# A late start for the second norm's spread over the partitions: behind the first half of FFN-in's first doubled pair

## The chip, the cores and the metric

One core of a Trainium2 chip runs the whole layer in one launch. The metric is the device time of one execution in microseconds. A profile shows one execution; its span runs from the first to the last instruction on the core, and the device time is a little longer than the span.

## The reference

One decoder layer, with 512 tokens of width 2048, in float32. The last part of it matters here:

```python
x = x + merged @ w_o[i]

h = rmsnorm(x, ffn_norm_g[i])
hid = h @ w_ffn_in[i]
gate = hid[..., :FFN_HIDDEN]
up = hid[..., FFN_HIDDEN:]
x = x + (jax.nn.silu(gate) * up) @ w_ffn_out[i]
```

`rmsnorm` divides each token by the root of its mean square and multiplies by a gain for each column. FFN_HIDDEN is 5632, so `w_ffn_in` is 2048 by 11264.

## The kernel before, in words

Everything lies transposed: the partitions hold model columns, the free dimension holds the 512 tokens. A float32 product is made of three products of rounded operands: each operand is split into a high part (ScalarE, L266 for activations and L334 for weights) and a low part, what the rounding left over (VectorE, L267 and L331). TensorE then multiplies high by high, high by low and low by high (`mm3`, L271 to L273).

A `Pair` (L572) is an output of 256 columns by 512 tokens. It comes in kinds. A **plain** pair multiplies eight operands of 256 rows ("forms", 0 to 7) with `mm3`, 12 matmuls for each form, into two PSUM banks, which L716 copies out. A **doubled** pair does the same job by a scheme with seven products instead of eight blocks: each product is one 512-column matmul of the high weights (L623, the activation's high and low halves side by side) and one 256-column matmul of the low weights (L625). Its weights come in four tiles of two forms each, 28 matmuls for each tile. It has seven PSUM accumulators: six banks named `ps` and one named `small`. `mix_doubled` (L671) adds the seven up on ScalarE and VectorE, at lines L680 and L683. There are two banks named `small`; the norm's work and the attention use them too.

Weights land by DMA in five landing buffers. SP's queue issues two loads for each weight tile (L316, L318), GpSimd's queue adds a third onto the first (L338, an accumulating load), VectorE makes two sums (L350), and the L334 and L331 splits write into one of three weight slots (`whi_76`, `whi_78`, `whi_80` and their `wlo`). A slot is written again when TensorE has done with it.

FFN-in has 44 pairs, `m` = 0 to 43 (L1302). Pair 0 is plain, pairs 1 to 43 are doubled. The forms of pair 0 are made while it runs: each is loaded from the spilled stream (L479, the transfer `wholes<-x`), multiplied by the gain (L483), and split for the plain pair (L266, L267), while L497 and two more splits make the further blocks that a doubled pair needs.

The norm's factor for each token is not applied to the forms but to the results: `hidden` (L1292) multiplies the gate half by `row2` (L1294), takes Silu (L1295), multiplies by the up half (L1297) and stores. `row2` is the factor of each token, the same in every partition. `Norm` (L861) makes it: squares are summed over the tiles, four small matmuls sum over the partitions (L882), VectorE and GpSimd make mean and power of minus one half (L887, L890), with the tokens on the partitions. Then `spread` (L849) turns these into a row in every partition: for each of four groups of 128 tokens VectorE writes a diagonal matrix (L854, two buffers), and TensorE multiplies it by ones (L856). L896 copies the PSUM bank to `row2`. A float32 matmul at L856 shows as two passes in the trace, so the four make eight.

The order is written by the recording program: `tick` (L198) runs after each group of matmuls, counts a clock, and runs whatever `after` (L192) has queued for that count. A `Staged` generator does one step at each tick. The scheduler then lays out each engine's instructions by priority and readiness. `norm2.row()` (L1305) ends whatever is left of the norm's steps at once.

Of the kernel before, what the change touches and what calls it, by code (L numbers as in the profile page):

```python
# [65 lines left out]
def hybrid_layer(  # L66
# [28 lines left out]
    def nm(s):  # L95
        return f"{s}_{next(names)}"
# [3 lines left out]
    class Block:  # L100
        def __init__(self, arena, start, n):
            self.arena, self.start, self.n = arena, start, n
# [8 lines left out]
    class Arena:  # L111
# [5 lines left out]
        def take(self, n, how="low"):  # L117


            spots = []  # L120
            for start, size in self.holes:
                end = start + size
                if how == "place":
                    start = -(-start // PLACE) * PLACE
                if end - start >= n:
                    if how == "high":
                        spots.append((-end, end - n))
                    elif how != "old":
                        spots.append((start, start))
                    else:  # L130
                        spots.extend((self.given[a // P : -(-(a + n) // P)].max(), a)
                                     for a in {*range(start, end - n + 1, 256), end - n})
            at = min(spots)[1]
            start, size = next(h for h in self.holes if h[0] <= at < h[0] + h[1])
            self.holes.remove((start, size))
            self.holes.extend(
                h for h in ((start, at - start), (at + n, start + size - at - n)) if h[1])
            return Block(self, at, n)

        def give(self, block):  # L140
            self.turns += 1
            self.given[block.start // P : -(-(block.start + block.n) // P)] = self.turns
            holes = sorted(self.holes + [(block.start, block.n)])
            self.holes = holes[:1]
            for s, n in holes[1:]:
                if sum(self.holes[-1]) == s:
                    self.holes[-1] = (self.holes[-1][0], self.holes[-1][1] + n)
                else:
                    self.holes.append((s, n))
# [26 lines left out]
    def small_bank():  # L176
        return psa.tile([P, T], F32, tag="small", name=nm("small"))
# [14 lines left out]
    def after(n, fn):  # L192
        heapq.heappush(waiting, (clock[0] + n, next(names), fn))
# [109 lines left out]
    class Weights:  # L303
# [20 lines left out]
        def steps(self):  # L324
            raw, c = self.blocks(self.land.f()), LANDED[self.kind]
            s = self.blocks(summed.f(), 2)

            def split(lo, blocks, r):
                h = self.hi[:, blocks]
                if lo:  # L330
                    in_turn(nc.vector.tensor_tensor(out=self.lo[:, blocks], in0=r,  # L331
                                                    in1=h.bitcast(F32), op=ALU.subtract))
                else:
                    in_turn(nc.scalar.activation(h, r, AF.Copy))  # L334

            def landed():
                if self.kind == "S":
                    nc.gpsimd.dma_start(out=raw[:, 3:5], in_=self.src[:, 1:3], accum_op=ALU.add)  # L338

            def high():  # L340
                self.slot = slots.popleft()
                self.hi, self.lo = (self.blocks(t, 7 if self.kind == "S" else 4)
                                    for t in self.slot)
                split(False, slice(0, c), raw)

            def sums():
                if self.kind == "S":
                    for o, x, y in ((s[:, 0], raw[:, 3], raw[:, 1]),
                                    (s[:, 1], s[:, 0], raw[:, 2])):
                        in_turn(nc.vector.tensor_tensor(out=o, in0=x, in1=y, op=ALU.add))  # L350

            def rest():
                split(True, slice(0, c), raw)
                if self.kind == "S":
                    split(False, slice(5, 7), s)
                    split(True, slice(5, 7), s)
                if spare[0] < 0:
                    spare[0] += 1
                    give(self.land)
                else:  # L360
                    landings.append(self.land)

            return landed, high, sums, rest
# [15 lines left out]
    def next_weights():  # L379
        ahead(1)  # L380
        return prepared.popleft().get()
# [20 lines left out]
    def doubles(kinds, at=0):  # L402

        k = 0
        while k < len(kinds):
            n = 2 if (at + k) % 2 == 0 and kinds[k : k + 2] in ("SS", "PP") else 1
            yield k, n
            k += n
# [325 lines left out]
    def pair(forms, last=False, plain=False, parts_done=None, at=0, home=lambda: None,  # L734
             doubled=False):

        kinds = "P" * len(forms) if plain else "".join(f.kind for f in forms)
        p = Pair(kinds, home, doubled)
        for k, n in doubles(kinds, at):
            slot, ws = next_weights()  # L740
            fs = forms[k : k + n]
            p.add("P" if plain else fs[0].kind, ws, [f.plain() if plain else f.get() for f in fs])
            for f in fs:
                if plain:
                    f.use_plain()
                if last:
                    f.free()
            slots.append(slot)
            if parts_done and k + n == kinds.find("P"):
                last_parts(p, forms[k + n :], parts_done)  # L750
                break
        return p

    def last_parts(p, forms, done):


        ws = [(f.get(), w) for k, n in doubles("P" * len(forms), len(GATE) - len(forms))
              for f, w in zip(forms[k : k + n], next_weights()[1])]
        y, z = p.ends()
        for ps, bs, a, b, c in ((y, (2, 3), 0, T, 0), (z[:, :256], (0, 1), 0, 256, T),  # L760
                                (bank()[:, :256], (0, 1), 256, T, T)):
            for u, ((xh, xl), (wh, wl)) in enumerate(ws):
                for k, i in enumerate(bs):
                    mm3(ps, wh[:, i], wl[:, i], xh[k][:, a:b], xl[k][:, a:b],
                        c + a > T and u + k == 0, k == 1 and u == len(ws) - 1)
            done(p.o, c + a, c + b, ps)
# [92 lines left out]


    class Norm:  # L861
        def __init__(self):
            self.acc = take(T)
            self.done = 0

        def add(self, raw):
            sq, acc = wide(), self.acc.f()
# [11 lines left out]
        def steps(self):  # L879
            ps = small_bank()  # L880
            for t in range(NT):
                nc.tensor.matmul(ps[:, t : t + 1], self.acc.f(t * P, (t + 1) * P), ones[:, 0:1],  # L882
                                 start=True, stop=True)
            give(self.acc)
            yield
            self.mean = consts.tile([P, NT], F32, name=nm("mean"))
            nc.vector.tensor_scalar(out=self.mean, in0=ps[:, :NT], scalar1=1.0 / D, scalar2=EPS,  # L887
                                    op0=ALU.mult, op1=ALU.add)
            self.cols = consts.tile([P, NT], F32, name=nm("cols"))
            nc.gpsimd.tensor_tensor(out=self.cols, in0=self.mean, in1=expo[:, :NT], op=ALU.pow)  # L890
            for _ in range(3):
                yield
            ps = spread(self.cols)
            yield
            self.block = take(T)
            nc.scalar.activation(self.block.f(), ps, AF.Copy)  # L896
            return self.block.f()
# [293 lines left out]
    for n, ((w, i), pr) in enumerate(zip(order, made())):  # L1191
# [6 lines left out]
        o = pr.out(block(w, i) if n < 3 else None)  # L1198
# [52 lines left out]
    give(norm1.block)  # L1251


    norm2 = Norm()
    spill = {(n, j): tc.dram_tile([P, 1024], F32, name=nm(n)) for n in ("x1", "sum", "x2")
             for j in range(KU)}
    there = set()
# [34 lines left out]
    def hidden(m, o):  # L1292
        g = o[:, :T]
        nc.vector.tensor_tensor(out=g, in0=g, in1=row2, op=ALU.mult)  # L1294
        nc.scalar.activation(g, g, AF.Silu)  # L1295
        yield
        nc.vector.tensor_tensor(out=g, in0=g, in1=o[:, T:], op=ALU.mult)  # L1297
        nc.sync.dma_start(out=spill["hid", m // 2][:, (m % 2) * T : (m % 2 + 1) * T], in_=g)
        if m % 2 == 1:
            there.add(("hid", m // 2))  # L1300

    for m in range(KH):  # L1302
        o = pair(fs, last=m == KH - 1, plain=m == 0, doubled=True).out()
        if m == 0:
            row2 = norm2.row()  # L1305
        st = Staged(hidden(m, o))
        st.step()
        if m == KH - 1:
            st.get()

# [29 lines left out]
    for j in range(KU):  # L1340
# [22 lines left out]
        else:  # L1363
            o = pair(gs, plain=j == 0).out()
# [90 lines left out]
```

## Time and profile before

| what | value |
|---|---|
| median of 3 runs | 2733.71 us |
| the three runs | 2729.75, 2733.71, 2735.45 us |
| profiled execution, device time | 2732.84 us |
| its span | 2731.1 us |
| granted TensorE clock, mean | 0.998 |
| instructions | 45752 |

TensorE is shown busy in nearly the whole span. Matmul durations in the trace include their drain (0.39 us for 512 columns), so the distance between the starts of two matmuls says how fast they go, not the duration. In the rows below, a number in square brackets is the idle time of the engine before the row, with what ended it.

### The profile page before, as it was taken

The page shows a single profiled execution, that of the slowest core. Times are in us where ns is not written, and L with a number is a line of the kernel's source. Part 1 is how long each engine was busy: PE and PEld are TensorE (multiplying, and loading weights), DVE is VectorE, ACT ScalarE, POOL GpSimd, SP SyncE. Part 2 cuts the span into 40 slices and gives each one's busy share as a digit, 9 for nine tenths or more (in the row PEclk, how much of TensorE's full clock was granted, in tenths as well). Part 3 has the DMA queues.
Part 4 walks back from the last instruction along what each step waited for, and adds up shares of the span by engine and source line. Part 5 has one row for each costly group of instructions (what it writes and reads, how often), then busy time and mean ns, then how long its engine had stood idle before and what let it go on. Part 6 is the DMA issues. An engine that isn't in the chain of part 4 may idle for free.

```text
span 2731.1 us, 45752 instructions
## 1 busy us (share of the span) xinstructions
PE 2703.8 (99%) x17243; PEld 2442.1 (89%) x17243; DVE 2073.4 (76%) x3377; ACT 1353.8 (50%) x2045; POOL 447.7 (16%) x527
## 2 busy tenths in 40 slices
PE   9999999999999999999999999999999999999999
PEld 7899999999998889988888888888888999989898
DVE  8566767677776567678888888888889567778776
ACT  7645556555554334364444444444445344453543
POOL 0222323232220000001111111111111111111110
PEclk9999999999999999999999999999999999999999
DMA  7677676777775457667888788888877659688784
GB/s 226 154 179 174 172 173 170 182 172 184 179 191 184 147 149 224 193 195 198 221 201 207 197 200 203 197 197 201 202 194 213 180 166 268 183 248 243 232 232 118
DMA packets 303134, 529.05 MB, mean 194 GB/s; under 512 B 25664, under 2 KB 162880, under 8 KB 302912
## 3 DMA queue, kind: packets, MB, share of 16 engines
q1 hardware_dynamic: 242160, 425.70, 49.0%
q0 software_dynamic: 60752, 100.43, 23.5%
q8 instruction: 135, 2.21, 0.3%
q14 instruction: 87, 0.71, 0.1%
HBM read 478.84 MB, written 47.19 MB: 193 GB/s over the span
## 4 chain that ended last, share of the span: by engine, by line
PE 93%; DMA 2%; DVE 2%; ACT 1%; issue 1%; POOL 0%; SPq 0%; ACTq 0%; DVEq 0%; POOLq 0%
PE ps L272 20%; PE ps L273 20%; PE ps L271 20%; PE ps L623 18%; PE ps L625 9%; PE small L623 3%; PE small L625 1%; PE small L1050 1%; PE small L942 1%; PE small L1026 1%; PE small L1003 1%; DMA wholes<-w_first 1%; DMA ple<-out 0%; DVE wlo L331 0%; DMA wholes<-x 0%
## 5 line engine op out<-in xcount | busy, mean ns | idle before, releaser
L271 PE MATMUL ps<-parts,whi 128*128 128x256 f32 (+1 forms) x3995 | 1245.0, 313 | 15.4 <-ACT parts L266 7.6
L334 ACT ACTIVATE whi<-wholes 128x512 fp32r<-128x512 f32 (+4 forms) x950 | 856.3, 917 | 792.5 <-PE ps L272 315.7
L272 PE MATMUL ps<-parts,whi 128*128 128x256 f32 (+1 forms) x3960 | 1229.8, 311 | 1.3 <-DVE parts L267 1.3
L273 PE MATMUL ps<-parts,wlo 128*128 128x256 f32 (+1 forms) x3960 | 1228.7, 310 | 0.1
L331 DVE TENSOR_TENSOR wlo<-wholes,whi 128x512 fp32r<-128x512 f32 (+4 forms) x950 | 964.1, 1048 | 154.9 <-ACT whi L334 153.5
L271 PEld LDWEIGHTS ps<-parts,whi 128*128 128x128 f32 x3995 | 763.4, 191 | 63.8 <-ACT parts L266 7.8
L272 PEld LDWEIGHTS ps<-parts,whi 128*128 128x128 f32 x3960 | 756.9, 191 | 44.8 <-DVE parts L267 2.2
L273 PEld LDWEIGHTS ps<-parts,wlo 128*128 128x128 f32 x3960 | 756.6, 191 | 39.2 <-DVE wlo L331 1.1
L623 PE MATMUL ps<-parts,whi 128*128 128x512 f32 x2064 | 739.0, 399 | 0.0
L625 PE MATMUL ps<-parts,wlo 128*128 128x256 f32 x2064 | 579.7, 281 | 0.0
L623 PEld LDWEIGHTS ps<-parts,whi 128*128 128x128 f32 x2064 | 387.8, 188 | 96.9
L625 PEld LDWEIGHTS ps<-parts,wlo 128*128 128x128 f32 x2064 | 389.9, 189 | 0.0
L350 DVE TENSOR_TENSOR wholes<-wholes 128x256 f32<-128x256 f32 (+1 forms) x794 | 328.2, 413 | 22.1 <-DMA wholes<-w_ffn_out 2.4
L338 POOL DMA_DIRECT2D wholes<-w_ffn_in x172 | 149.7, 870 | 699.2 <-DVE wholes L350 266.6
L338 POOL DMA_DIRECT2D wholes<-w_in x132 | 117.3, 891 | 516.0 <-DMA wholes<-w_in 248.1
L683 DVE TENSOR_TENSOR out<-out,ps 128x256 f32<-128x256 f32 x258 | 107.2, 416 | 94.5 <-ACT out L680 94.4
L652 DVE TENSOR_TENSOR out<-out 128x256 f32<-128x256 f32 x59 | 25.0, 424 | 180.6 <-ACT out L649 180.3
L267 DVE TENSOR_TENSOR parts<-wholes,parts 128x1024 fp32r<-128x1024 f32 (+4 forms) x131 | 123.6, 952 | 13.9 <-ACT parts L266 13.6
L623 PE MATMUL small<-parts,whi 128*128 128x512 f32 x344 | 131.2, 399 | 0.0
L266 ACT ACTIVATE parts<-wholes 128x1024 fp32r<-128x1024 f32 (+4 forms) x131 | 105.6, 834 | 38.9 <-DVE wholes L497 18.1
L338 POOL DMA_DIRECT2D wholes<-w_ffn_out x56 | 57.0, 1036 | 401.8 <-DMA wholes<-w_ffn_out 190.3
L1295 ACT ACTIVATE out<-out 128x512 f32<-128x512 f32 x44 | 27.8, 633 | 165.4 <-DVE out L1294 165.4
(119 smaller groups left out, 1666.9 us busy)
## 6 DMA issues: line engine op xcount, KB each, us to landing
wholes<-w_ffn_in SPq DMA_DIRECT2D x172, 384.0 KB, 5.4
wholes<-w_in SPq DMA_DIRECT2D x132, 384.0 KB, 4.8
wholes<-w_ffn_in SPq DMA_DIRECT2D x172, 256.0 KB, 4.6
wholes<-w_ffn_in POOLq DMA_DIRECT2D x172, 256.0 KB, 5.2
wholes<-w_in SPq DMA_DIRECT2D x132, 256.0 KB, 3.9
wholes<-w_in POOLq DMA_DIRECT2D x132, 256.0 KB, 4.8
wholes<-x SPq DMA_DIRECT2D x32, 512.0 KB, 5.3
wholes<-w_ffn_out SPq DMA_DIRECT2D x31, 512.0 KB, 4.3
```

The lines of the kernel that those rows point to most:

```text
L266: return (nc.scalar.activation(hi, src, AF.Copy), nc.vector.tensor_tensor(out=lo, in0=src, in1=hi.bitcast(F32), op=ALU.subtract))
L267: nc.vector.tensor_tensor(out=lo, in0=src, in1=hi.bitcast(F32), op=ALU.subtract))
L271: nc.tensor.matmul(ps[:, s], sh, mh[:, s], start=start, stop=False)
L272: nc.tensor.matmul(ps, sh, ml, start=False, stop=False)
L273: return nc.tensor.matmul(ps, sl, mh, start=False, stop=stop)
L331: in_turn(nc.vector.tensor_tensor(out=self.lo[:, blocks], in0=r, in1=h.bitcast(F32), op=ALU.subtract))
L334: in_turn(nc.scalar.activation(h, r, AF.Copy))
L338: nc.gpsimd.dma_start(out=raw[:, 3:5], in_=self.src[:, 1:3], accum_op=ALU.add)
L350: in_turn(nc.vector.tensor_tensor(out=o, in0=x, in1=y, op=ALU.add))
L623: nc.tensor.matmul(ps, wh[:, w], t[:, x].rearrange("p s c -> p (s c)"), start=first, stop=False)
L625: mark(nc.tensor.matmul(ps[:, :256], wl[:, w], t[:, x, 0], start=False, stop=last))
L683: in_turn(nc.vector.tensor_tensor(out=out, in0=x, in1=y, op=op))
```

## The change

The second norm is made with `held=True`, and its generator stops ahead of `spread` for as long as that holds. It is let go by `first_out`, four ticks after pair 0 has been read out. `row2` and the first step of `hidden` for pair 0 follow there.

```diff
     class Norm:
-        def __init__(self):
+        def __init__(self, held=False):
             self.acc = take(T)
-            self.done = 0
+            self.done, self.held = 0, held
...
             for _ in range(3):
                 yield
+            while self.held:
+                yield
             ps = spread(self.cols)
...
-    norm2 = Norm()
+    norm2 = Norm(held=True)
...
+    def first_out():
+        nonlocal row2
+        norm2.held = False
+        row2 = norm2.row()
+        st.step()
+
+    row2 = None
     for m in range(KH):
         o = pair(fs, last=m == KH - 1, plain=m == 0, doubled=True).out()
+        st = Staged(hidden(m, o))
         if m == 0:
-            row2 = norm2.row()
-        st = Staged(hidden(m, o))
-        st.step()
+            after(4, first_out)
+        else:
+            st.step()
```

The engines' orders in the two built programs are the same up to the old place of the spread and again from the end of pair 1 on; instructions and addresses are the same there. Between the two, TensorE's order is (shortened; names without numbers; T1 to T4 are the four weight tiles of pair 1):

```
before                                     changed
pair 0, forms 0, 1 (24 matmuls)            pair 0, forms 0, 1 (24)
L856 x2, one L271, L856 x2                 -
pair 0, forms 2 to 7 (72)                  pair 0, forms 2 to 6 (60)
                                           pair 1, T1: one L623
                                           pair 0, form 7: two L271
                                           pair 1, T1: L625, L623, ... (8)
                                           pair 0, form 7: the other ten
pair 1, T1 (28)                            pair 1, T1: the other 19
pair 1, T2 (28)                            pair 1, T2 (28)
                                           L856 x2, T3: one L623, L856 x2
pair 1, T3, T4                             pair 1, T3 (its L625 next), T4
```

On ScalarE, the two L334 of T2 stood behind form 7's first L266 and stand ahead of it in the changed program (L483 x2, L334 x2, L266). On VectorE, T2's two L331 likewise stand ahead of form 7's first L267. The four L854 stand behind the L331 of T4, with an L350 behind the first and another behind the second. The store of pair 0's hidden half moves on SP's queue behind two more sets of weight loads.

## Prediction, made before the changed kernel ran

> **What bounds the kernel now.** I read the page first, then the stretches around the change, then the engines' orders there in time.
>
> ```profile
> span 2731.1 us, 45752 instructions
> PE 2703.8 (99%) x17243; PEld 2442.1 (89%) x17243; DVE 2073.4 (76%) x3377; ACT 1353.8 (50%) x2045; POOL 447.7 (16%) x527
> ```
>
> TensorE sets the end: whatever it waits for here is added to the time, whatever it stops waiting for is taken off, until a place where it waits for something else. Its busy share counts drains, so the speed is read from the starts of matmuls. The first fence of starts is the plain pair, then the first doubled one:
>
> ```profile
> 1217.28 0.39 PE L271 MATMUL ps<-parts,whi 128*128 128x512 f32 x1
> ...
> 1225.44 0.39 PE L271 MATMUL ps<-parts,whi 128*128 128x512 f32 x1
> 1225.67 0.48 PE L272 MATMUL ps<-parts,whi 128*128 128x512 f32 x1
> ...
> 1228.30 0.39 PE L623 MATMUL ps<-parts,whi 128*128 128x512 f32 x1
> ...
> 1238.18 0.40 PE L623 MATMUL ps<-parts,whi 128*128 128x512 f32 x1
> ```
>
> 36 matmuls lie between the first two rows: 8.16/36 = 0.227 us for each of 512 columns. Between the last two lie two weight tiles of 28 matmuls: 9.88/28 = 0.353 us for a couple of L623 and L625. The row at 1225.44 is the first matmul of form 7, the last form of pair 0; 1228.30 is the first of T1 (pair 1's first weight tile), 1238.18 the first of T3.
>
> What the spread costs at its old place:
>
> ```profile
> 1210.15 0.39 PE L273 MATMUL ps<-parts,wlo 128*128 128x512 f32 x1
> 1210.38 0.60 PE L856 MATMUL small<-diag,ones 128*128 128x128 f32 x4
> 1210.74 0.48 PE L271 MATMUL ps<-parts,whi 128*128 128x512 f32 x1
> 1211.47 0.71 PE L856 MATMUL small<-diag,ones 128*128 128x128 f32 x4 [0.25 <-DVE diag L854]
> 1211.94 0.48 PE L272 MATMUL ps<-parts,whi 128*128 128x512 f32 x1
> 1212.25 0.40 PE L273 MATMUL ps<-parts,wlo 128*128 128x512 f32 x1
> ```
>
> From 1210.15 to 1212.25 are 2.10 us, in which three matmuls would have taken 0.68: the spread costs **1.42 us** of TensorE. Half a microsecond of it is the wait for the third diagonal, which VectorE made late behind a split:
>
> ```profile
> 1210.00 1.22 DVE L267 TENSOR_TENSOR parts<-wholes,parts 128x1024 fp32r<-128x1024 f32 x1
> 1211.14 0.47 DVE L854 TENSOR_SCALAR diag<-ident,cols 128x128 f32<-128x128 f32 x2
> ```
>
> **The change part by part.**
>
> *Removed at the old place:* 1.42 us of TensorE. Without more, form 7 would be reached at 1225.44 - 1.42 = 1224.02.
>
> *What is late next: form 7.* Its raw tile comes by DMA:
>
> ```profile
> 1213.76 0.42 SPq L479 DMA_DIRECT2D wholes<-x  x1
> 1221.88 1.34 ACT L483 ACTIVATE wholes<-wholes,gcol 128x512 f32<-128x512 f32 x2 [2.22 <-DMA wholes<-x]
> 1223.25 1.06 ACT L266 ACTIVATE parts<-wholes 128x1024 fp32r<-128x1024 f32 x1
> 1224.22 1.77 ACT L334 ACTIVATE whi<-wholes 128x1280 fp32r<-128x1280 f32 x2
> 1224.39 1.22 DVE L267 TENSOR_TENSOR parts<-wholes,parts 128x1024 fp32r<-128x1024 f32 x1
> 1225.52 2.09 DVE L331 TENSOR_TENSOR wlo<-wholes,whi 128x1280 fp32r<-128x1280 f32 x2
> 1225.90 1.44 ACT L266 ACTIVATE parts<-wholes 128x768 fp32r<-128x768 f32 x3
> ```
>
> and the stretch in which it was under way (after the engines: granted clock, DMA share, GB/s):
>
> ```profile
> 1213.00:1220.00 7.00, 7.00 (x32) 5.78 (x31) 3.74 (x7) 2.65 (x5) 1.75 (x2) 1.00 1.07 347
> ```
>
> The tile was asked for at 1213.76 and landed at 1221.88, in a stretch where the DMA engines were busy all the time (share 1.07, 347 GB/s). This does not follow TensorE: nothing that the change removes lies ahead of that load except 1.1 us of VectorE work, and the split that releases the two loads in front of it waits for ScalarE anyway. I take 1221.88 as it is. Already before, TensorE came 0.2 us too early: the L272 above at 1225.67 starts when VectorE's L267 (1224.39 + 1.22) is done. So of the 1.42 us at most that much could have been won if nothing else were touched.
>
> The changed order is worse there. ScalarE does L483, then both L334 of T2, and only then form 7's high split. L334 takes 1.68 us from start to the next start (1224.22 to 1225.90) and can follow L483 at 1223.15, so L266 runs from 1224.85 to 1225.9. TensorE's order is one product of T1, then form 7's two L271. It reaches the first of these at 1224.02 + 0.23 = 1224.25, finds no high part, and stands until 1225.95: **1.7 us of waiting**, for what was 0.2. The T1 products that lie behind in its order are ready and can't go first. VectorE's low split of form 7 is behind T2's two L331: these can follow L334's first half at about 1224.45 and take 2.0, then L267 1.22, done at 1227.65. TensorE asks for it after two L271 and four couples, 1225.95 + 0.45 + 1.41 = 1227.8: no wait.
>
> *On to the new place.* From 1225.95 twelve matmuls of form 7 (2.72), 27 couples and one L625 (9.65) are left ahead of T3: 1238.3. I add 0.15 for a bank: pair 1's sixth accumulator takes over pair 0's second bank, which is copied out behind the two L334 of T3, here as before:
>
> ```profile
> 1228.27 1.88 ACT L334 ACTIVATE whi<-wholes 128x1280 fp32r<-128x1280 f32 x2 [0.45 <-PE ps L272]
> 1230.06 0.58 ACT L716 ACTIVATE out<-ps 128x512 f32<-128x512 f32 x1
> 1230.65 1.28 ACT L1295 ACT_TABLE_LOAD   x1
> 1231.95 0.63 ACT L1295 ACTIVATE out<-out 128x512 f32<-128x512 f32 x1
> ```
>
> In the new order the L334 start when pair 0's last L272 drains (1230.0), the copy ends 1.79 + 0.58 later, at 1232.4, and TensorE wants the bank at 1232.3. So T3 is reached at **1238.45**, against 1238.18 before.
>
> *The spread at the new place.* The rows that make it:
>
> ```profile
> L854 DVE TENSOR_SCALAR diag<-ident,cols x12: 278/280/389, 69.4 to 2578.0; 128x128 f32<-128x128 f32 x12
> L856 PE MATMUL small<-diag,ones x24: 270/275/377, 76.3 to 2579.4; 128*128 128x128 f32 x24
> 1234.20 2.09 DVE L331 TENSOR_TENSOR wlo<-wholes,whi 128x1280 fp32r<-128x1280 f32 x2
> 1236.54 0.88 DVE L350 TENSOR_TENSOR wholes<-wholes 128x256 f32<-128x256 f32 x2
> ```
>
> VectorE has the first diagonal behind T4's L331. With form 7 and T3's splits 1 us later than before, I get these L331 from 1234.7 to 1236.75 (before: the third row, 1234.20 to 1236.29), and diagonals 1 and 2, with an L350 of 0.34 between, by 1237.6. TensorE, at 1238.45, need not wait. The first two L856 take 0.36 (1210.38 to 1210.74), the L623 0.23. Diagonal 3 has to wait for the first L856 to read its buffer (two buffers, as before), about 0.37 after it starts; then 0.28 for itself and some 0.05 for each of two signals: ready at 0.75, when TensorE has been at 0.59 for a moment; diagonal 4 follows at 0.95, the last L856 takes 0.18, and the weights behind it come some 0.08 late, as at 1212.25. That is 1.2 us, of which 0.23 is the L623: **0.97 us**. Bounds: 0.9 without a wait (0.36 + 0.47 + 0.08, from the old place), 1.42 as it was. I take 0.97, since the late split on VectorE is gone, but the hand-over of the diagonals is not.
>
> *Behind the new waits.* While VectorE waits for the third diagonal's buffer, the L331 of pair 2's first tile (2.0 us) stand behind it, wanted only after T3 and T4, 9.9 us later. ScalarE's copy to `row2`, the table load and Silu end near 1242.3; behind them stands an L334 that waits for T3's last products anyway, near 1243.8: hidden, 1.5 us to spare. The store of the hidden half leaves SP near 1243.5 instead of 1233.97; its buffer is wanted again by pair 2's sums, over 10 us on. GpSimd's queue has its loads in the same order. These go at nothing.
>
> **Sum.** 0.27 us late at T3, and 0.97 for the spread: **+1.24 us**. Behind that everything follows TensorE as before. The profiled execution took 2732.84 us (span 2731.1 and 1.7 around it), so 2734.1. The median of the three runs lies 0.9 above the profiled execution (range 2729.75 to 2735.45); from there the same sum is 2734.95. A difference below 0.2% (5.5 us) is about what can't be told from no change here.
>
> **The rivals.**
>
> *Form 7 is in time.* If its tile lands 1.7 us earlier in most executions, the wait at its L271 is gone, and the change only exchanges 1.42 for 0.97: -0.45, and -0.2 for the wait that was there before: 2732.2. For it: other executions differ by 5 us. Against it: the DMA share over 1 at a fixed place. 18%.
>
> *VectorE is late at the new place.* The diagonals now stand behind T4's splits and an L350, with 0.85 us to spare by my sum. If the chain through form 7 is later by 1 to 3 us, TensorE stands at L856 for the excess of it, one for one: about +1 more, 2735.1 and up to 2736.5. 12%.
>
> *Slower: the tile lands later and TensorE cools.* T1's splits come 1.4 us earlier, so SP sends the next two weight loads at 1218.6 and not at the row below, while form 7's tile is still on its way:
>
> ```profile
> 1220.08 0.38 SPq L316 DMA_DIRECT2D wholes<-w_ffn_in  x1
> 1202.63 0.39 PE L273 MATMUL ps<-parts,wlo 128*128 128x512 f32 x1
> 1203.87 0.50 PE L271 MATMUL ps<-parts,whi 128*128 128x512 f32 x1 [0.85 <-ACT out L802]
> ```
>
> The two are 640 KB, at 347 GB/s 1.9 us; at worst the tile is that much later, and TensorE's gap grows from 1.7 to 3.6 us. The trace's own gap of 0.85 us, at 1203, left the next matmuls at 0.23 apart; no gap of this stage is longer. If from about twice that on the clock is halved for as long as the gap lasted, 1.8 to 3.6 us of matmuls are lost again, say 2.6: 1.24 + 1.9 + 2.6 = +5.7, 2738.5. [...] 8%.
>
> That the spread isn't where it is meant to be is ruled out by the built order.
>
> **How the numbers follow.** Forecast 62%, 2734.1, by itself 2732.5 to 2736. The rivals add 2732.2 below and 2738.5 above; the runs' own spread is -4.0 and +1.7 about their median. Eight times in ten: 2730.5 to 2738.5. Beyond 0.2% lie only the slower rival's upper half and runs that scatter: faster 0.04, same 0.89, slower 0.07.
>
> **What would show it.** In the changed profile: form 7's first L271 with about 1.7 us of idle time, released by ScalarE's L266; L334 between L483 and L266; the eight L856 near 1239 with a wait below 0.3 us and no L267 ahead of the third diagonal; the granted clock at 1.00; T3's next products at 0.35 us a couple. Wrong would be: the tile `wholes<-x` landing elsewhere than near 1222, idle time at the first L856, or a change of idle time anywhere behind 1245.

## The result, and the profile after

| | before | after |
|---|---|---|
| median | 2733.23 us of 20 runs (2728.1 to 2738.55) | 2727.74 us of 20 runs (2716.0 to 2737.29) |
| ratio after / before | | 0.9974, 95% interval 0.9962 to 0.9985 |
| profiled execution | 2732.84 us | 2727.78 us |

The changed kernel is 0.26% faster where 0.05% slower was forecast, and the time lies below the range. The second thing to see in the table is the scatter: 10 us for the kernel before, 21 us for the changed one, with six of its twenty executions between 2716 and 2719.1 and only one more below 2725.

The span and L623, the 512-column product of a couple, on the page of after:

```profile
span 2726.1 us, 45750 instructions
L623 PE MATMUL ps<-parts,whi 128*128 128x512 f32 x2064 | 726.7, 392 | 0.0
```

and L623 on the page of before:

```profile
L623 PE MATMUL ps<-parts,whi 128*128 128x512 f32 x2064 | 739.0, 399 | 0.0
```

The number of these instructions is the same, no idle time stands on either line (the last column), and yet L623 takes 392 ns instead of 399. Only the starts of matmuls tell what that is worth. The timeline answers three places of each kernel: the last L273 ahead of the old place of the spread (for before it stands in the prediction, 1210.15), the first L623 of pair 2, and the last L623 of FFN-in. Before:

```profile
1248.07 0.40 PE L623 MATMUL ps<-parts,whi 128*128 128x512 f32 x1
2078.76 0.40 PE L623 MATMUL small<-parts,whi 128*128 128x512 f32 x1
```

After:

```profile
1213.98 0.39 PE L273 MATMUL ps<-parts,wlo 128*128 128x512 f32 x1
1255.26 0.39 PE L623 MATMUL ps<-parts,whi 128*128 128x512 f32 x1
2070.36 0.39 PE L623 MATMUL small<-parts,whi 128*128 128x512 f32 x1
```

- Up to the old place this execution is 3.83 us later than that of before. Nothing is changed there: it is scatter of the earlier stages.
- From there to pair 2 before took 37.92 us, after 41.28. So the stretch that the change touches became **3.36 us longer**; the forecast was +1.24.
- From pair 2 to the end of FFN-in before took 830.69 us and after 815.10: **15.6 us shorter**, in a stretch where both kernels issue the same instructions in the same order. FFN-in has 2408 couples of L623 and L625 (2064 + 344, the 344 into the small bank), 14 to a weight tile and 56 to a pair; 2351 of them lie between these rows. 830.69/2351 = 0.3533 us for a couple, 815.10/2351 = 0.3467.
- Behind FFN-in the lead shrinks from 8.4 to 5.0 us (the spans), again in work that nothing changed.

The 15.6 us don't come in one place. A window of before (time, busy time and number of instructions of each engine, granted clock, DMA share, GB/s):

```profile
1250.00:1500.00 250.00, 250.00 (x1418) 216.78 (x1416) 219.69 (x394) 117.34 (x163) 43.52 (x50) 1.00 0.83 207
```

and two of after:

```profile
1250.00:1500.00 250.00, 250.00 (x1444) 220.68 (x1443) 222.48 (x400) 121.00 (x169) 44.37 (x51) 1.00 0.83 209
1750.00:2000.00 250.00, 250.00 (x1445) 220.66 (x1444) 222.58 (x401) 120.43 (x168) 45.29 (x52) 1.00 0.83 206
```

TensorE is busy 250 us of 250 and has a granted clock of 1.00 in all three, and does 1444 matmuls in the one kernel and 1418 in the other. Busy share and clock hide the difference; the count shows it.

In the timeline the two look like this. Before:

```profile
1300.01 0.40 PE L623 MATMUL ps<-parts,whi 128*128 128x512 f32 x1
1300.25 0.28 PE L625 MATMUL ps<-parts,wlo 128*128 128x256 f32 x1
1300.37 0.40 PE L623 MATMUL ps<-parts,whi 128*128 128x512 f32 x1
...
1301.07 0.40 PE L623 MATMUL ps<-parts,whi 128*128 128x512 f32 x1
```

After:

```profile
1299.98 0.39 PE L623 MATMUL ps<-parts,whi 128*128 128x512 f32 x1
1300.21 0.28 PE L625 MATMUL ps<-parts,wlo 128*128 128x256 f32 x1
1300.33 0.39 PE L623 MATMUL ps<-parts,whi 128*128 128x512 f32 x1
...
1301.02 0.39 PE L623 MATMUL ps<-parts,whi 128*128 128x512 f32 x1
```

From the first row to the last are three couples: 1.06 us before, 1.04 after. In nanoseconds, before repeats every three couples: from an L623 to its L625 241, 236, 233, and from there to the next L623 120, 113, 117; 353 a couple. After is even, 230 and 117, 347 a couple. I call them the **slow** and the **quick rhythm**. Before has the slow one in all of its couples; after has it through T2 and the quick one from the spread on (a few couples of T1 ran at 347 ns too).

That gives the theory to test (R): the couples have two stable rhythms; which one runs is set by the last thing that disturbed the stream, and it then lasts for hundreds of couples. The spread's last matmuls, in front of a 256-column product, turned it. Rivals: the long stall at form 7 turned it (C); any small matmul in the stream would (P); the gain comes from the place that the spread left (W).

### The profile page after: what moved, and what is told of

Its sections match the earlier page's. It is cut to its first block, busy times and chain, and to the rows that moved or that the text cites. A ratio compares the mean times of both kernels' runs of the same rounds, so it can differ in the third digit from the quotient of the medians.

```text
span 2726.1 us, 45750 instructions
## 1 busy us (share of the span) xinstructions
PE 2691.6 (99%) x17243; PEld 2443.3 (90%) x17243; DVE 2072.4 (76%) x3377; ACT 1353.3 (50%) x2045; POOL 448.3 (16%) x527
## 4 chain that ended last, share of the span: by engine, by line
PE 90%; issue 3%; DMA 2%; DVE 2%; ACT 1%; POOL 1%; SPq 0%; DVEq 0%; ACTq 0%; POOLq 0%
PE ps L273 19%; PE ps L272 19%; PE ps L271 19%; PE ps L623 17%; PE ps L625 9%; PE small L623 3%; PE small L625 1%; DVE wlo L331 1%; DMA wholes<-x 1%; PE small L1052 1%; PE small L1028 1%; PE small L1005 1%; PE small L944 1%; ACT whi L334 0%; DMA wholes<-w_in 0%
## 5 line engine op out<-in xcount | busy, mean ns | idle before, releaser
L271 PE MATMUL ps<-parts,whi 128*128 128x256 f32 (+1 forms) x3995 | 1247.5, 314 | 18.5 <-ACT parts L266 10.2
L334 ACT ACTIVATE whi<-wholes 128x512 fp32r<-128x512 f32 (+4 forms) x950 | 855.6, 917 | 782.0 <-PE ps L272 307.8
L272 PE MATMUL ps<-parts,whi 128*128 128x256 f32 (+1 forms) x3960 | 1231.8, 311 | 1.3 <-DVE parts L267 1.3
L273 PE MATMUL ps<-parts,wlo 128*128 128x256 f32 (+1 forms) x3960 | 1230.5, 311 | 1.7 <-DVE wlo L331 1.5
L331 DVE TENSOR_TENSOR wlo<-wholes,whi 128x512 fp32r<-128x512 f32 (+4 forms) x950 | 964.0, 1049 | 157.8 <-ACT whi L334 156.3
L271 PEld LDWEIGHTS ps<-parts,whi 128*128 128x128 f32 x3995 | 764.4, 191 | 68.1 <-ACT parts L266 11.1
L272 PEld LDWEIGHTS ps<-parts,whi 128*128 128x128 f32 x3960 | 758.0, 191 | 44.8 <-DVE parts L267 2.4
L273 PEld LDWEIGHTS ps<-parts,wlo 128*128 128x128 f32 x3960 | 757.8, 191 | 40.8 <-DVE wlo L331 2.7
L623 PE MATMUL ps<-parts,whi 128*128 128x512 f32 x2064 | 726.7, 392 | 0.0
L625 PE MATMUL ps<-parts,wlo 128*128 128x256 f32 x2064 | 579.6, 281 | 0.0
L623 PEld LDWEIGHTS ps<-parts,whi 128*128 128x128 f32 x2064 | 386.7, 187 | 84.5 <-ACT out L716 0.3
L625 PEld LDWEIGHTS ps<-parts,wlo 128*128 128x128 f32 x2064 | 391.3, 190 | 0.1
L350 DVE TENSOR_TENSOR wholes<-wholes 128x256 f32<-128x256 f32 (+1 forms) x794 | 329.0, 414 | 27.7 <-DMA wholes<-w_ffn_out 4.6
L683 DVE TENSOR_TENSOR out<-out,ps 128x256 f32<-128x256 f32 x258 | 107.5, 417 | 77.9 <-ACT out L680 77.8
L267 DVE TENSOR_TENSOR parts<-wholes,parts 128x1024 fp32r<-128x1024 f32 (+4 forms) x131 | 123.7, 954 | 16.0 <-ACT parts L266 15.7
L623 PE MATMUL small<-parts,whi 128*128 128x512 f32 x344 | 128.8, 391 | 0.0
L266 ACT ACTIVATE parts<-wholes 128x1024 fp32r<-128x1024 f32 (+4 forms) x131 | 105.5, 834 | 42.2 <-DVE wholes L497 16.7
```

Source lines behind the costliest of these rows:

```text
L266: return (nc.scalar.activation(hi, src, AF.Copy), nc.vector.tensor_tensor(out=lo, in0=src, in1=hi.bitcast(F32), op=ALU.subtract))
L267: nc.vector.tensor_tensor(out=lo, in0=src, in1=hi.bitcast(F32), op=ALU.subtract))
L271: nc.tensor.matmul(ps[:, s], sh, mh[:, s], start=start, stop=False)
L272: nc.tensor.matmul(ps, sh, ml, start=False, stop=False)
L273: return nc.tensor.matmul(ps, sl, mh, start=False, stop=stop)
L623: nc.tensor.matmul(ps, wh[:, w], t[:, x].rearrange("p s c -> p (s c)"), start=first, stop=False)
```

## The experiments

All times are medians, with the range and the number of executions, beside runs of before on the same chip. Lines inserted into the kernels move the couple's L623 and L625 to L633 and L637 (or a line or two off). The small matmul of the experiments is

```
def tap():
    nc.tensor.matmul(small_bank()[:, :P], ones, ident, start=True, stop=True)
```

and nothing reads its result; everything else is computed as before. `self.number` counts the doubled pairs from 1, `self.tile` a pair's weight tiles from 0; i is the product, u the couple in it.

**1. One small matmul in front of a 256-column product, in the kernel before.**

```diff
                         nc.tensor.matmul(ps, wh[:, w], t[:, x]...)
+                        if self.number == 1 and self.tile == 2 and i == 0 and u == 0:
+                            tap()
                         mark(nc.tensor.matmul(ps[:, :256], wl[:, w], t[:, x, 0], ...))
```

> The kernel before with the spread at its old place and one more small matmul (128 columns, ident and ones into a spare bank, its result unread), put between the first 512-column product and the first 256-column product of the third tile of the first doubled pair. Theory R (the couples of the doubled product have two rhythms, 353 and 347 ns, and a small matmul in front of a 256-column product puts them into the quick one for the rest of FFN-in): 347 ns per couple from that place on, no stall at form 7 beyond 0.2 us, no half clock there; 2733.2 - 15.7 + 0.2 = about 2718 us. Rival C (the quick rhythm comes from the 2.2 us stall and the half clock at form 7, which this kernel does not have): 353 ns, 2733.5 us. Rival W (the gain comes from taking the spread out of the stretch behind the plain pair): 353 ns, 2733.5 us.

Measured: 2727.97 us (2719.43 to 2730.49, 8 runs; before 2733.49), ratio 0.9975 (0.9965 to 0.9985). The spread is at its old place, and the rhythm turns at the small matmul (L575, two records of it), which the timeline has between an L633 and its L637:

```profile
1238.40 0.40 PE L633 MATMUL ps<-parts,whi 128*128 128x512 f32 x1
1238.63 0.38 PE L575 MATMUL small<-ident,ones 128*128 128x128 f32 x2
1238.77 0.36 PE L637 MATMUL ps<-parts,wlo 128*128 128x256 f32 x1
1238.97 0.40 PE L633 MATMUL ps<-parts,whi 128*128 128x512 f32 x1
```

Ahead of it the couples have 241, 236 and 233 ns from L633 to L637, behind it 230 each. One operation that computes nothing of use makes the kernel 5.5 us faster. In this execution TensorE waits at form 7 too, 0.37 us at its first L271 and 0.80 at its first L272, so the forecast of no wait there beyond 0.2 us missed; but the couples behind that wait run slow until the small matmul. So neither the wait at form 7 (C) nor the place that the spread left (W) is what turned the rhythm here. But the size was missed, 2728 instead of 2718, and two windows say why:

```profile
1250.00:1570.00 320.00, 320.00 (x1848) 282.16 (x1847) 286.08 (x514) 153.63 (x213) 56.55 (x65) 1.00 0.83 209
1600.00:2070.00 470.00, 470.00 (x2662) 407.60 (x2662) 412.69 (x740) 224.05 (x310) 80.03 (x92) 1.00 0.80 198
```

924 couples in 320 us are 0.346, 1331 in 470 us are 0.353: the quick rhythm was lost between. The place:

```profile
1581.15 0.47 PE L633 MATMUL ps<-parts,whi 128*128 128x512 f32 x1
1581.45 0.28 PE L637 MATMUL ps<-parts,wlo 128*128 128x256 f32 x1
```

Couple 1017 takes 0.30 us from its L633 to its L637, where those ahead of it take 0.23, and behind it the slow rhythm runs to the end. In every profiled execution, that of before too, VectorE loses 0.2 us once, near couple 849 or 1017. Its rows show it just ahead of the couple, here of before, one pair earlier and at that couple:

```profile
1565.21 0.41 DVE L683 TENSOR_TENSOR p<-p,ps 128x256 f32<-128x256 f32 x1
1565.55 0.41 DVE L683 TENSOR_TENSOR out<-out,ps 128x256 f32<-128x256 f32 x1
...
1584.99 0.42 DVE L683 TENSOR_TENSOR p<-p,ps 128x256 f32<-128x256 f32 x1
1585.53 0.42 DVE L683 TENSOR_TENSOR out<-out,ps 128x256 f32<-128x256 f32 x1
```

The second L683 usually follows the first by 0.34 us, here once by 0.54, with no wait that the trace shows. That this is what makes the couple late is inferred: the two stand at the same place in each of the nine executions that run at 347 ns there. In the slow rhythm TensorE loses nothing by it; in the quick one it loses 0.08 us and may fall back to the slow one.

**2. The same small matmul one place earlier, in front of the 512-column product.**

> The same kernel with the small matmul one place earlier, in front of the 512-column product. Theory R (only in front of a 256-column product does it change the rhythm): 353 ns per couple, 2733.5 us. Rival P (any interruption of the doubled stream does it): 347 ns from there on, about 2718 us. Rivals C and W: 353 ns, 2733.5 us.

Measured: 2732.38 us (2727.71 to 2735.35, 11 runs), ratio 0.9993 (0.9984 to 1.0002); 1417 matmuls in 250 us throughout. No turn: that any small matmul does it (P) is out as it stands. At which phase of the rhythm one in front of 512 columns might do it wasn't tried.

**3. The spread one step earlier, its last matmuls in front of a 512-column product.**

```diff
-            after(4, first_out)
+            after(3, first_out)
```

> The changed kernel with the spread released one step earlier, so that its four matmuls stand in the second tile of the first doubled pair: one in front of a 256-column product, one in front of a 512-column product, and the last two in front of a 512-column product. Theory R, with the last interruption deciding: back to 353 ns per couple, and what is left is the stall and the half clock at form 7, +3.3 us: about 2736.5 us. Rival P: 347 ns, 2733.2 - 15.7 + 3.3 = about 2721 us. Rival C: 347 ns, about 2721 us. Rival W: 347 ns, about 2721 us.

Measured: 2731.93 us (2722.04 to 2737.95, 12 runs), ratio 0.9991 (0.9978 to 1.0003). Its profiled execution ran at 347 ns from the spread to couple 1017 and at 353 from there, so both forecasts missed: the last interruption, in front of 512 columns, did not bring back the slow rhythm, nor did the quick one last. It was a third pattern, two couples of 343 and 350 ns, with the same mean of 347.

**4. The changed kernel again.**

> The changed kernel again, nothing edited. Every theory: 2716 to 2737 us, median 2728. Theory R says of the profiled execution that its time follows the stretch in which the couples take 347 ns: about 2721 us where all couples from the third tile of the first doubled pair on take 347 ns and all other stages run as in the kernel before, and some 0.0065 us more for every couple that takes 353 ns. Rival C: the same, but from the stall at form 7 on, so from the first tile of the pair.

Measured: 2720.99 us (2711.42 to 2736.97, 12 runs), ratio 0.9963 (0.9947 to 0.9979). Seven executions lie at or below 2721.1, five at or above 2730, none between. The profiled one is of the second kind (2736.97 us), and its window (L623 is back at 399 ns, too) is that of before:

```profile
1250.00:1500.00 250.00, 250.00 (x1417) 216.88 (x1416) 220.01 (x395) 118.12 (x163) 43.49 (x50) 1.00 0.83 207
```

So the same program runs in the one rhythm or the other, and with the slow one the change costs time. This execution has the long wait at form 7 as well (1.81 us idle) and stays slow, which speaks against C once more. A time by itself doesn't tell the rhythm: the profiled one of the first twenty executions, 2727.78 us, ran quick to the end of FFN-in, but had lost 3.8 us ahead of the change and loses 1.7 to the clock. What the other executions did between couples is not shown.

**5 to 8. More places.** Number 5 has the small matmul in pairs 1, 16 and 19 (behind couples 849 and 1017), number 6 once in pair 3, number 7 in pair 1 in front of 256 columns and in pair 4 in front of 512, number 8 is the changed kernel with three of them.

```diff
-if self.number == 1 and self.tile == 2 and i == 0 and u == 0:
+if self.number in (1, 16, 19) and self.tile == 2 and i == 0 and u == 0:          # 5
+if self.number == 3 and self.tile == 1 and i == 4 and u == 1:                    # 6
+if self.number == 4 and self.tile == 2 and i == 0 and u == 0:    # 7, beside that of 1, ahead of the 512
+if (self.number, self.tile) in ((1, 3), (16, 2), (19, 2)) and i == 0 and u == 0: # 8, in the changed kernel
```

> The kernel before with the small matmul between the two products of a couple at three places: the third tile of the doubled pairs 1, 16 and 19 (behind the couples 849 and 1017, at which the rhythm fell back in earlier executions). Theory R: 347 ns per couple from the first place to the end of FFN-in, but for at most some 20 couples behind couple 849 or 1017: 2733.5 - 15.4 + 0.6 = about 2718.5 us, in nearly every execution. Rival C (the stall at form 7 makes the quick rhythm) is out already; rival T (the time follows the arrival at form 7 and not the couples): 2727 us as with one matmul.

> The small matmul once, but elsewhere: third doubled pair, second tile, between the two products of the last couple but three. Theory R, if every place in front of a 256-column product does: 353 ns up to there, 347 ns from there to couple 849 or 1017, then 353 or 347: 2725 to 2728 us. If only the place at a tile's first couple does (rival F): 353 ns throughout, 2733.7 us.

> Two small matmuls: in front of a 256-column product in doubled pair 1, third tile, and in front of a 512-column product in doubled pair 4, third tile. If the last interruption decides the rhythm: 347 ns for 168 couples, then 353 ns: 2733.5 - 1.1 + 0.4 = about 2732.8 us. If one in front of a 512-column product leaves the rhythm as it is: 347 ns up to couple 849 or 1017, 2725 to 2728 us.

> The changed kernel (spread in the first doubled pair's third tile) with the small matmul between the products of a couple in the fourth tile of pair 1 and in the third of pairs 16 and 19. Theory R with the stall at form 7 as a cost of its own (+2 to +3 us): 347 ns to the end of FFN-in in nearly every execution, 2718.5 + 2.5 = about 2721 us, 2 to 3 us above the kernel with the three small matmuls and the spread at its old place. Rival W (taking the spread out of the stretch behind the plain pair is worth something by itself): not above that kernel, 2718.5 us or less.

Measured, against 2733.03 for before: number 5 2723.02 us (2711.94 to 2729.89, 7 runs), ratio 0.9953 (0.9934 to 0.9972); number 6 2728.56 (2717.27 to 2736.19, 12 runs), 0.9979 (0.9968 to 0.9990); number 7 2726.69 (2724.08 to 2730.09, 6 runs), 0.9974 (0.9963 to 0.9985); number 8 2720.89 (2715.57 to 2730.31, 6 runs), 0.9954 (0.9939 to 0.9968).

Number 6 shows that another place does as well. In number 7 the small matmul ahead of the 512 columns left the mean of 347 ns as it was (x1445 in the window 1250:1500), but turned the even couples into the pattern of experiment 3, 343 and 350 in turn; couple 1017 brought back the slow rhythm. Number 8's time came out as forecast, the comparison did not: it lies 2.1 us below number 5, not 2 to 3 above. So the times leave open whether taking the spread out of its old place is worth something by itself (W). In the traces the stretch from the old place to pair 2 takes 39.38 us in number 8 and 38.09 in number 5. Number 5 missed: in its profiled execution couple 1017 brought the slow rhythm back, and the small matmul in pair 19 did not turn it:

```profile
1586.69 0.40 PE L633 MATMUL ps<-parts,whi 128*128 128x512 f32 x1
1586.93 0.38 PE L575 MATMUL small<-ident,ones 128*128 128x128 f32 x2
1587.07 0.36 PE L637 MATMUL ps<-parts,wlo 128*128 128x256 f32 x1
```

Here it follows 0.24 us behind its L633, in experiment 1 0.23 us: it stands in the couple that has 241 ns (240 in this one), there in that of 233. So the theory needed the phase: which of the three couples is hit.

**9 and 10. The phase.** Experiment 1, one couple and two couples later.

```diff
-if ... i == 0 and u == 0:
+if ... i == 0 and u == 1:     # 9
+if ... i == 1 and u == 0:     # 10
```

> One small matmul as in the first experiment, but one couple later (second couple of the third tile of pair 1, again in front of its 256-column product). The slow rhythm repeats every three couples (starts 241 and 120, 236 and 113, 233 and 117 ns apart). In the first experiment the small matmul stood behind the 512-column product of 233, in another one behind that of 236: both turned the rhythm; in a third it stood behind that of 240 and nothing turned. Theory R by phase (where in the three couples it falls decides): here it falls behind 241: 353 ns throughout, 2733.5 us. Rival R without phase (in front of any 256-column product): 347 ns to couple 849 or 1017, 2725 to 2728 us.

> The same another couple later (third couple of the tile). Theory R by phase: it falls behind the 512-column product of 236, which turned the rhythm once: 347 ns to couple 849 or 1017, 2725 to 2728 us. If only 233 turns it surely: 353 ns, 2733.5 us. Rival without phase: 2725 to 2728 us.

Measured, against 2733.8 for before: number 9 2736.43 us (2720.97 to 2741.26, 11 runs, one of them below 2731), ratio 1.0003 (0.9991 to 1.0015); number 10 2725.32 (2718.99 to 2731.97, 6 runs), 0.9970 (0.9958 to 0.9982). Their windows, number 9 first:

```profile
1250.00:1500.00 250.00, 250.00 (x1417) 216.68 (x1417) 219.41 (x393) 117.64 (x163) 43.97 (x51) 1.00 0.81 208
```

```profile
1250.00:1500.00 250.00, 250.00 (x1444) 220.44 (x1443) 222.47 (x401) 120.05 (x168) 44.47 (x51) 1.00 0.84 212
```

The three kernels 1, 9 and 10 differ by one couple in the place of one matmul, and go quick, slow, quick as the phase foretold.

**11. A version for speed.** Two small matmuls, two couples apart, at pairs 16 and 19: one of them must meet a phase that turns.

```diff
+SPOTS = ((1, 2, 0, 0), (16, 2, 0, 0), (16, 2, 1, 0), (19, 2, 0, 0), (19, 2, 1, 0))
-if self.number == 1 and self.tile == 2 and i == 0 and u == 0:
+if (self.number, self.tile, i, u) in SPOTS:
```

> A version for speed: the kernel before with the spread at its old place, one small matmul in pair 1 as in the first experiment, and two each, two couples apart, in the third tiles of pairs 16 and 19, so that one of the two meets a phase that turns the rhythm if it has fallen back. Theory R by phase: 347 ns to the end of FFN-in in nearly every execution, 2733.5 - 15.4 + 1.1 = about 2719 us, with few executions above 2724. If the second of two can turn it back to the slow one: 2723 us as with single ones.

Measured: **2716.9 us** (2712.65 to 2720.81, 5 runs; before 2733.8), ratio 0.9940 (0.9928 to 0.9951), and no execution above 2721. It beats both kernels. The profiled execution fell back at couple 1017; the first small matmul of pair 19 fell into a couple of 240 ns and didn't turn it, the second did. The window behind it:

```profile
1750.00:2000.00 250.00, 249.98 (x1442) 219.55 (x1441) 222.13 (x401) 120.40 (x168) 44.50 (x51) 1.00 0.81 203
```

## Why the prediction was wrong

**The step that failed** is the last: "Behind that everything follows TensorE as before", with 0.353 us for a couple taken as a constant of the hardware. The runs show that it is one of two values, and that what I added up decides between them. With 0.347 instead of 0.353 the 2351 couples behind the change give -15.6 us, over four times what the change costs at its place. I had divided 9.88 by 28 and thought the quotient a property of the products; the uneven starts in the same timeline (0.23 and 0.24, 0.11 and 0.12) were there to be seen. Of my own three signs of being wrong, the third, "a change of idle time anywhere behind 1245", didn't cover it either: no idle time changed, only the distance of starts. The "0.35 us a couple" that I named as a sign of being right is too coarse to tell 0.353 from 0.347. Nor is the quick rhythm a steady effect of the change: the profiled execution of after has it and that of experiment 4 does not. That the seven short executions of experiment 4 have it is likely by their times, but not shown. A median of the changed kernel depends on how many executions fall into which group.

**Form 7's tile: right in kind, too small.** The timeline of after at that place:

```profile
1227.81 0.39 PE L623 MATMUL ps<-parts,whi 128*128 128x512 f32 x1
1230.22 0.89 PE L271 MATMUL ps<-parts,whi 128*128 128x512 f32 x2 [2.03 <-ACT parts L266]
1230.91 0.41 PE L625 MATMUL ps<-parts,wlo 128*128 128x256 f32 x1
1231.56 0.41 PE L625 MATMUL ps<-parts,wlo 128*128 128x256 f32 x1
```

and ScalarE ahead of it:

```profile
1226.21 1.34 ACT L483 ACTIVATE wholes<-wholes,gcol 128x512 f32<-128x512 f32 x2 [4.05 <-DMA wholes<-x]
1227.45 1.78 ACT L334 ACTIVATE whi<-wholes 128x1280 fp32r<-128x1280 f32 x2
1229.13 1.04 ACT L266 ACTIVATE parts<-wholes 128x1024 fp32r<-128x1024 f32 x1
```

The L334 stands between L483 and L266 as forecast. The wait is 2.41 - 0.23 = 2.2 us instead of 1.7, 0.5 of it because the tile came later: L483 starts 12.23 us behind the last L273 ahead of the spread's old place, before 11.73. I had taken the landing as fixed. That the change made it later isn't shown: in the four traces with the changed order there (after, experiments 3, 4 and 8) L483 starts 11.77 to 12.23 us behind that L273, in the nine with the spread at its old place 11.58 to 13.30.

**The clock: wrong.** I kept the clock at 1.00 for that wait, an estimate that no run had shown. In the rows above a couple takes 0.65 us behind the wait, and the window there has

```profile
1230.60:1234.10 3.50, 3.50 (x12) 2.92 (x11) 3.50 (x7) 0.92 (x3) 0.00 (x0) 0.51 0.89 211
```

a granted clock of 0.51 for 3.5 us: 1.7 us lost. This is what my slower rival foresaw; it counted on a wait of 3.6 us, and it came at 2.2, above the "about twice that" (1.7 us) from which the rival let the clock fall. The forecast's own wait of 1.7 us lay at that limit, and I gave that no price. The rival's 2.6 us, from a clock halved for as long as the gap lasts, was an estimate too and is shown by no run: in the runs it is 3.5 us at 0.51 behind 2.03 us of idle time here, and 3.4 us at 0.50 behind 1.79 us in before, 1.7 us lost each time. In experiment 4 the wait was almost the same and the clock stayed:

```profile
1224.36 0.39 PE L623 MATMUL ps<-parts,whi 128*128 128x512 f32 x1
1226.55 0.74 PE L271 MATMUL ps<-parts,whi 128*128 128x512 f32 x2 [1.81 <-ACT parts L266]
...
1226.00:1231.00 5.00, 4.45 (x22) 3.79 (x23) 4.51 (x8) 2.65 (x6) 0.07 (x1) 1.00 0.79 181
```

Behind 2.03 us of idle time the clock was 0.51, behind 1.81 us 1.00, but the length alone doesn't decide. The trace of before already had a drop, behind FFN-in:

```profile
2081.05 0.47 PE L271 MATMUL ps<-parts,whi 128*128 128x512 f32 x1 [1.79 <-DVE out L683]
2082.10:2085.50 3.40, 3.40 (x10) 2.63 (x9) 3.40 (x6) 1.78 (x2) 0.00 (x0) 0.50 0.66 222
```

Experiment 1 has the same idle time at the same place, and the clock stays:

```profile
2075.01 0.47 PE L271 MATMUL ps<-parts,whi 128*128 128x512 f32 x1 [1.79 <-DVE out L695]
2072.50:2080.00 7.50, 5.71 (x27) 4.53 (x26) 7.10 (x16) 5.35 (x6) 0.00 (x0) 1.00 0.70 225
```

So the 1.7 us that the clock took were bad luck of this execution, and a forecast with a wait of about 2 us should have given them a chance.

**The spread at its new place: right, a little small.**

```profile
1244.46 0.61 PE L856 MATMUL small<-diag,ones 128*128 128x128 f32 x4
1244.82 0.47 PE L623 MATMUL ps<-parts,whi 128*128 128x512 f32 x1
1245.22 0.71 PE L856 MATMUL small<-diag,ones 128*128 128x128 f32 x4
1245.89 0.40 PE L623 MATMUL ps<-parts,whi 128*128 128x512 f32 x1
```

1245.89 - 1244.46 - 0.35 (the couple in it) = 1.08 us, forecast 0.97, with 1.42 at the old place. T3 was reached 30.48 us behind that last L273, before 28.03: +2.45, which is the 0.27 of the forecast, the 0.5 of the tile and the 1.7 of the clock. 2.45 + 1.08 - 0.18 for 27 couples that already ran at 347 gives 3.35, as measured (3.36). In the execution of experiment 4, with the slow rhythm and a full clock, two rows

```profile
1210.53 0.39 PE L273 MATMUL ps<-parts,wlo 128*128 128x512 f32 x1
1250.24 0.40 PE L623 MATMUL ps<-parts,whi 128*128 128x512 f32 x1
```

give 39.71 against 37.92: **+1.79 us** for the change by itself, where I had 1.24.

**The rivals.** None of them spoke of the couples. "Form 7 in time" fell with the wait, "VectorE late" with the 1.08; the tile that came later and the clock did come, the tile with 0.5 us where I had 1.9, the clock with 1.7 where I had 2.6. That the tile came later because of other loads, as the rival had it, isn't shown.

**What stays open.** Why the stream has two rhythms isn't shown: the trace gives the starts of matmuls and weight loads, not what sets the distance between them. Nor is it settled why the changed kernel's spread turned the rhythm in after and not in experiment 4. Two things differ: the second group of L856, whose diagonal comes late, starts 0.44 us behind its L623 in experiment 4 and 0.40 in after, and the couple just ahead of the spread has 235 ns there and 232 in after, so that the spread meets another phase. Neither was changed by itself. In experiment 8 the couples ran at 347 ns before the spread came. The phase foretells what a small matmul does, but not what other disturbances do: at the 11th and 12th couple of pair 1 a loss of 0.17 us left experiments 3 and 4 in the slow rhythm and took experiment 8 out of it, into couples of 343 and 350.

## What to carry to other kernels

Where TensorE is busy 99% and the trace shows no idle time, compare the number of matmuls in equal windows, or the distance of starts, before and after a change: a stream of unequal products can run at two speeds (here 353 and 347 ns a couple), and a small disturbance far upstream can decide which for the next thousand (in experiment 1 from couple 29 to 1017). If the time of a kernel falls into two groups, look for such a state before weighing the change, and test it with an operation that does nothing, moved one place at a time. What a change costs at its own place is still to be worked out row by row, but its sum is good only as long as the rate behind it is shown to be the same.

## What the runs showed of the hardware

- Couples of a 512- and a 256-column product with weight loads of 128 columns run at 353 or at 347 ns, at the same granted clock of 1.00, for hundreds of couples each (in experiment 1 924 of them in 320 us, then 1331 in 470). Those at 347 are even (230 and 117) or come as 343 and 350 in turn (experiments 3, 7, 8).
- A matmul of 128 columns between the two products turned the slow rhythm in each of the seven profiled cases in which it fell into the couple of 233 or of 236 ns (experiments 1, 5, 6, 7, 10 and twice in 11), and in none of the three in that of 241 (5, 9, 11). Among couples at 347 ns such matmuls left the mean as it was (5, 7, 8, 11). In number 7 one in front of 512 columns turned even couples into those of 343 and 350, in number 8 one in front of 256 did the reverse.
- VectorE lost 0.2 us once in FFN-in in every profiled execution (0.54 us between two L683 instead of 0.34), without a wait in the trace: near couple 849 in after and experiments 4 and 8, near couple 1017 in the other ten. In the quick rhythm TensorE lost 0.08 us there; the slow rhythm came back in six of seven cases at 1017 and in neither of two at 849.
- The granted clock was 0.51 for 3.5 us behind 2.03 us of idle time of TensorE (after, form 7) and 0.50 for 3.4 us behind 1.82 us (after) and 1.79 us (before), both behind FFN-in. It stayed at 1.00 behind 1.79 us (experiment 1) and 1.81 us (experiment 4).
